# A column roll of an 8192 x 8192 matrix: which of the last rows are copied as half rows

## The chip, the cores and the metric

The kernel runs on one core of one Trainium2 chip. The metric is the device time of one execution in microseconds (us), taken as the median over several executions; lower is better. A profiled execution also leaves a page and a trace, from which the busy times, waits and DMA records here are read.

## The reference

The matrix is float32, 268 MB, and every row is rotated to the right by 100 columns:

```python
def setup_inputs():
    return {
        "x": np.random.randn(8192, 8192).astype(np.float32),
        "shift": 100,
    }

def reference(x: np.ndarray, shift: int) -> np.ndarray:
    return np.roll(x, shift, axis=1)
```

So `out[r, 100:] = x[r, :8092]` and `out[r, :100] = x[r, 8092:]`. Nothing is computed; the kernel only moves data, 268 MB read and 268 MB written.

## The kernel before

With a shift of 100 the kernel sets `a = 256` and `g = a - s = 156` (lines 20 to 23). Output columns from 256 on go one way, the first 256 columns another.

*The wide part (lines 34 to 43).* Columns 256 to 8191 of the output are copied straight from DRAM to DRAM. The rows are viewed as 128 blocks `c` of 64 rows; a block's rows are numbered by `e` (16) and `j` (4), and a DMA takes one `c` and one `j`: sixteen rows, four rows apart, each a contiguous run of 7936 floats (31,744 bytes, "a whole row" in this text). Such a DMA moves 496 KB. Even `j` are issued on SP's queue, odd `j` on ACT's (`engines[j % 2]`, lines 25 and 43), two DMAs per block on each.

In the last four blocks, 256 rows, line 40 cuts the columns at `mid = (256 + 8192) // 256 * 128 = 4224`, and each group of sixteen rows goes as two DMAs of 3968 columns (15,872 bytes per row, 248 KB per DMA: "half rows"), one after the other on the same queue:

```python
for c in range(blocks):
    parts = ((a, mid), (mid, n_cols)) if c >= blocks - 4 and a < mid else ((a, n_cols),)
    for j in range(4):
        for lo, hi in parts:
            engines[j % 2].dma_start(out=om[c, j, :, lo:hi], in_=xm[c, j, :, lo - s:hi - s])
```

Each queue issues 248 whole-row and 16 half-row DMAs. The framework gives each queue four semaphores, which it uses in turn, and lets a DMA wait until the one that used its semaphore before has landed: each queue has at most four DMAs in flight, and the one issued fifth waits for the first. A DMA of sixteen rows puts one row on each of the sixteen DMA engines; its semaphore is full when all sixteen have marked their row complete.

*The edge part (lines 60 to 80).* The first 256 output columns are gathered in SBUF: for 16 groups of 512 rows, GpSimd's queue loads the pieces from both ends of the rows (lines 72, 73, 76), the vector engine copies them into place (lines 74, 77), and GpSimd's queue stores them (line 80). Nothing links this part to the wide part but the DMA engines, which both use.

At the end SP waits for all outstanding DMAs, and the engines meet at closing barriers.

Of the kernel before, what the change touches and what calls it, by code (L numbers as in the profile page):

```python
# [1 line left out]

# [4 lines left out]


@with_exitstack
def kernel(  # L10
    ctx: ExitStack,
    tc: tile.TileContext,
    x: bass.AP,
    shift: int,
    out: bass.AP,
):
    nc = tc.nc
    n_rows, n_cols = x.shape
    s = shift % n_cols
    a = -(-s // 128) * 128  # L20
    if 0 < a <= 384 and a + 128 <= n_cols:
        a += 128
    g = a - s
    P = nc.NUM_PARTITIONS
    engines = [nc.sync, nc.scalar]
    n_chunks = 16
    rows = n_rows // n_chunks

    xm = x.rearrange("(c e j) w -> c j e w", e=16, j=4)
    om = out.rearrange("(c e j) w -> c j e w", e=16, j=4)
    if a < n_cols:
        blocks = n_rows // 64
        mid = (a + n_cols) // 256 * 128
        for c in range(blocks):
            parts = ((a, mid), (mid, n_cols)) if c >= blocks - 4 and a < mid else ((a, n_cols),)  # L40
            for j in range(4):
                for lo, hi in parts:
                    engines[j % 2].dma_start(out=om[c, j, :, lo:hi], in_=xm[c, j, :, lo - s:hi - s])
    if a == 0:
        return


    if a > 512:
        for i in range(n_chunks):
            r = slice(i * rows, (i + 1) * rows)  # L50
            nc.gpsimd.dma_start(out=out[r, :s], in_=x[r, n_cols - s:])
            if g > 0:
                nc.gpsimd.dma_start(out=out[r, s:a], in_=x[r, :g])
        return

    Q = 4  # L60
    n_st = n_rows // (P * Q)
    reads = ctx.enter_context(tc.tile_pool(name="reads", bufs=n_st))
    heads = ctx.enter_context(tc.tile_pool(name="heads", bufs=n_st))
    xt = x.rearrange("(k p q) c -> k p q c", q=Q, p=P)
    ot = out.rearrange("(k p q) c -> k p q c", q=Q, p=P)
    tiles = []
    for k in range(n_st):
        t = reads.tile([P, Q - 1, a], x.dtype)
        h = heads.tile([P, Q, a], x.dtype)
        lead = bass.AP(tensor=x.tensor, offset=(k * P * Q + 1) * n_cols - s,  # L70
                       ap=[[Q * n_cols, P], [n_cols, Q - 1], [1, a]])
        nc.gpsimd.dma_start(out=t[:], in_=lead)  # L72
        nc.gpsimd.dma_start(out=h[:, Q - 1, :s], in_=xt[k, :, Q - 1, n_cols - s:])  # L73
        nc.vector.tensor_copy(h[:, :Q - 1, :s], t[:, :, :s])  # L74
        if g > 0:
            nc.gpsimd.dma_start(out=h[:, 0, s:], in_=xt[k, :, 0, :g])  # L76
            nc.vector.tensor_copy(h[:, 1:, s:], t[:, :, s:])  # L77
        tiles.append(h)
    for k, h in enumerate(tiles):
        nc.gpsimd.dma_start(out=ot[k, :, :, :a], in_=h[:])  # L80


# [1 line left out]
_INS = ['x', 'shift']  # L84
_OUTS = [((8192, 8192), 'float32')]

_NUMBERS = {'shift': 100}


# [26 lines left out]
```

## Time and profile before

| what | value |
|---|---|
| median of 4 runs | 828.56 us (828.01, 828.45, 828.67, 831.01) |
| the profiled execution's own time | 828.13 us |
| its span, first to last instruction | 826.3 us |
| HBM read and written | 268.44 MB each |
| busy: GpSimd, vector engine | 41.1 us, 12.0 us |
| last issue of the edge part's stores | 401 us |
| issue of one DMA on SP's queue, on ACT's | 0.51 us, 0.52 us |
| first half-row DMA issued, last one | 793.3 us, 819.7 us |

The profiled execution is one run of the program, and its own time is 1.8 us above its span. The page shows the load of the DMA engines as tenths per fortieth of the span, and per stretch as a share: 1.00 means that all sixteen are moving data all the time. The GB/s beside it count each byte once, as read from its source. The trace holds a record of each packet that a DMA engine moved (here a packet is a row or a half row), with its start, duration, queue and size, and for each DMA sixteen completion marks, one from each DMA engine.

### The profile page before, as it was taken

To read this page: it belongs to the slowest core of one execution; us is meant where nothing else is said; L and a number is where in the kernel's file an instruction comes from. 1 tells how busy PE (TensorE), PEld (TensorE's weight loads), DVE (VectorE), ACT (ScalarE), POOL (GpSimd) and SP (SyncE) were. 2 spreads that over 40 slices of the span, in tenths; PEclk is the share of its full clock that TensorE was granted. 3 is DMA by queue.
4 is the path that set the end of the run, shared out by engine and by line. 5 is a ranking of instruction groups with operands and counts; after the bars stand their busy time and mean duration, and the time that the engine had idled before them with its cause. 6 is when DMAs were issued, how large, how long until landed. Compare 5 with 4: busy or idle time off the path is not lost. (4 is left out here: it accounts for less than half of the span.)

```text
span 826.3 us, 689 instructions
## 1 busy us (share of the span) xinstructions
DVE 12.0 (1%) x32; POOL 41.1 (5%) x68
## 2 busy tenths in 40 slices
DVE  0000000000000000000000000000000000000000
POOL 2001100010011000000000000000000000000000
DMA  9999999999999999999999999999999999999998
GB/s 305 349 328 354 346 343 335 345 336 343 343 342 351 354 350 351 349 346 350 345 353 339 325 328 332 329 327 335 323 335 318 331 322 337 326 321 333 327 310 288
DMA packets 22277, 276.90 MB, mean 335 GB/s; under 512 B 9472, under 2 KB 9728, under 8 KB 13824
## 3 DMA queue, kind: packets, MB, share of 16 engines
q1 hardware_dynamic: 8448, 130.04, 46.3%
q10 hardware_dynamic: 8448, 130.04, 44.5%
q0 software_dynamic: 5376, 16.78, 8.3%
q14 instruction: 5, 0.04, 0.0%
HBM read 268.44 MB, written 268.44 MB: 650 GB/s over the span
## 5 line engine op out<-in xcount | busy, mean ns | idle before, releaser
L80 POOL DMA_DIRECT2D out_dram<-h x16 | 11.4, 713 | 143.6 <-DMA out_dram<-h 84.5
L76 POOL DMA_DIRECT2D h<-in_x_dram x16 | 8.7, 541 | 148.1 <-DMA t<-in_x_dram 148.1
L72 POOL DMA_DIRECT2D t<-in_x_dram x16 | 12.2, 760 | 29.2 <-DMA h<-in_x_dram 28.3
L73 POOL DMA_DIRECT2D h<-in_x_dram x16 | 8.9, 558 | 40.3 <-DMA h<-in_x_dram 40.3
L74 DVE COPY h<-t 128x300 f32<-128x300 f32 x16 | 5.9, 367 | 277.0 <-DMA t<-in_x_dram 277.0
L77 DVE COPY h<-t 128x468 f32<-128x468 f32 x16 | 7.5, 468 | 0.0
L97 POOL MEMSET const-float32-0.0<- 128x1 f32 x1 | 0.1, 98 | 0.2 <-issue 0.2
L97 POOL MEMSET const-bfloat16-1.0<- 128x1 bf16 x1 | 0.1, 101 | 0.0
L97 POOL MEMSET const-uint8-127<- 128x1 uint8 x1 | 0.1, 99 | 0.0
L97 POOL MEMSET const-float32-1.0<- 128x1 f32 x1 | 0.1, 98 | 0.0
## 6 DMA issues: line engine op xcount, KB each, us to landing
out_dram<-in_x_dram ACTq DMA_DIRECT2D x248, 496.0 KB, 12.7
out_dram<-in_x_dram SPq DMA_DIRECT2D x248, 496.0 KB, 12.7
out_dram<-h POOLq DMA_DIRECT2D x16, 512.0 KB, 97.9
t<-in_x_dram POOLq DMA_DIRECT2D x16, 384.0 KB, 51.3
out_dram<-in_x_dram SPq DMA_DIRECT2D x16, 248.0 KB, 6.0
out_dram<-in_x_dram ACTq DMA_DIRECT2D x16, 248.0 KB, 6.0
h<-in_x_dram POOLq DMA_DIRECT2D x16, 78.0 KB, 43.2
h<-in_x_dram POOLq DMA_DIRECT2D x16, 50.0 KB, 50.0
```

Source lines behind the costliest of these rows:

```text
L72: nc.gpsimd.dma_start(out=t[:], in_=lead)
L73: nc.gpsimd.dma_start(out=h[:, Q - 1, :s], in_=xt[k, :, Q - 1, n_cols - s:])
L74: nc.vector.tensor_copy(h[:, :Q - 1, :s], t[:, :, :s])
L76: nc.gpsimd.dma_start(out=h[:, 0, s:], in_=xt[k, :, 0, :g])
L77: nc.vector.tensor_copy(h[:, 1:, s:], t[:, :, s:])
L80: nc.gpsimd.dma_start(out=ot[k, :, :, :a], in_=h[:])
L97: nc = _bacc.Bacc("TRN2", target_bir_lowering=False, num_devices=1)
```

## The change

Half rows are kept for the last two groups of sixteen rows alone: in the last block, for `j` of 2 (SP's queue) and 3 (ACT's queue). Blocks 124 to 126 and `j` of 0 and 1 in block 127 go as whole rows. Columns, rows per DMA, queues and the edge part are as before. Each queue now issues 255 whole-row and 2 half-row DMAs.

```diff
         for c in range(blocks):
-            parts = ((a, mid), (mid, n_cols)) if c >= blocks - 4 and a < mid else ((a, n_cols),)
             for j in range(4):
+                last = c == blocks - 1 and j >= 2 and a < mid
+                parts = ((a, mid), (mid, n_cols)) if last else ((a, n_cols),)
                 for lo, hi in parts:
                     engines[j % 2].dma_start(out=om[c, j, :, lo:hi], in_=xm[c, j, :, lo - s:hi - s])
```

## The prediction

> **What bounds the kernel now.** I read the busy shares and the forty slices first, then the queues and issues, then the waits of the SP queue, then a table of stretches over the end, and last the packet and completion records of the trace.
>
> ```profile
> span 826.3 us, 689 instructions
> DVE 12.0 (1%) x32; POOL 41.1 (5%) x68
> DMA  9999999999999999999999999999999999999998
> ...
> q1 hardware_dynamic: 8448, 130.04, 46.3%
> q10 hardware_dynamic: 8448, 130.04, 44.5%
> q0 software_dynamic: 5376, 16.78, 8.3%
> ```
>
> No compute engine is above 5%, and the sixteen DMA engines are busy in every slice: the kernel is a copy, bound by what these engines move. q1 and q10 are the hardware queues of SP and ACT and carry 130 MB each; q0, GpSimd's, has only the edge columns and lands its last store at 510.9 us, long before the rows that the change touches.
>
> ```profile
> out_dram<-in_x_dram ACTq DMA_DIRECT2D x248, 496.0 KB, 12.7
> out_dram<-in_x_dram SPq DMA_DIRECT2D x248, 496.0 KB, 12.7
> out_dram<-in_x_dram SPq DMA_DIRECT2D x16, 248.0 KB, 6.0
> out_dram<-in_x_dram ACTq DMA_DIRECT2D x16, 248.0 KB, 6.0
> ```
>
> A whole-row DMA lands 12.7 us after its issue, a half-row one after 6.0 us. Each has sixteen rows, one per DMA engine. Each queue keeps four in flight: an issue waits for the landing of the DMA four earlier on its queue. The SP issue at 793.33 us, for one, follows by 0.02 us the last of the sixteen completion marks of the DMA on whose semaphore it waits.
>
> ```profile
> engine line waited for: us in total, times, longest us
> SPq L43 <- DMA out_dram<-in_x_dram: 18.1, 14, 2.5
> SPq L111 <- DMA out_dram<-in_x_dram: 5.2, 4, 2.2
> ```
>
> These are the SP queue's waits from 795 to 827 us. A DMA counts as landed when the slowest engine has done its row, so that engine sets the pace of issue, and faster ones eat into what they still have queued.
>
> ```profile
> 700.00:780.00 80.00, 0.00 (x0) 0.00 (x0) 1.00 1.00 326
> 780.00:800.00 20.00, 0.00 (x0) 0.00 (x0) 1.00 1.00 327
> 800.00:805.00 5.00, 0.00 (x0) 0.00 (x0) 1.00 0.83 276
> 805.00:810.00 5.00, 0.00 (x0) 0.00 (x0) 1.00 0.94 330
> 810.00:815.00 5.00, 0.00 (x0) 0.00 (x0) 1.00 0.97 318
> 815.00:820.00 5.00, 0.00 (x0) 0.00 (x0) 1.00 0.96 333
> 820.00:823.00 3.00, 0.00 (x0) 0.00 (x0) 1.00 1.00 328
> 823.00:824.00 1.00, 0.00 (x0) 0.00 (x0) 1.00 0.58 222
> 824.00:825.00 1.00, 0.00 (x0) 0.00 (x0) 1.00 0.08 32
> ```
>
> The last two columns are DMA share and GB/s. Whole rows run at share 1.00 and 326 to 327 GB/s. Where half rows take over there is a dip (0.83, 276 GB/s), then a share of 0.94 to 0.97 at nearly the old rate, then a drain of about one microsecond.
>
> The sixteen completion marks of each DMA explain the dip. For the DMA that landed at 793.31 us, the marks stand before the last one by 7.2, 5.2, 4.9 ... 2.0, 1.7 and 0 us, 3.7 us on the mean. I call this the mean lag: how far the slowest engine is behind the average. From 500 to 795 us it lies between 3.5 and 5.6 us, mean 4.3. Under half rows it shrinks, since what a queue holds for an engine is halved and the fast engines run empty while the slowest catches up: 1.7 us on the mean after 800 us, 0.90 us for the last DMA, which lands at 825.38 us. The span ends 0.97 us later, after the closing barriers.
>
> **The change, part by part.** Blocks 124 to 126 and the first two row groups of block 127 become whole rows. That removes 28 half-row DMAs and adds 14 whole ones; 4 half ones stay, one pair at the end of each queue.
>
> *Issues.* Each queue issues 7 fewer DMAs of 0.51 us, 3.6 us in all. They lie beside the movement of bytes: SP alone waited 18.1 us for landings in that stretch. Worth 0 as long as landings set the pace; were that cover gone, the saving would be 3.6 us at the most, but the wait row excludes it.
>
> *Packets.* A whole row's packet took 1.546 us on the mean from 700 to 795 us (979 packets, shortest 1.173), a half row's 0.736 us (512 packets, shortest 0.589). Twice the half is 1.47 us, so a whole row is no cheaper per byte; it looks 0.07 us dearer. Fourteen rows per engine change: 14 x 0.074 = 1.0 us if that is a property of size, 0 if it comes from fewer engines being active at a time (shares of 0.94 to 0.97). The rates, 326 against 318 to 333, speak for the second; I take 0 and keep 1.0 for the range.
>
> *The dip goes.* From 800 to 823 us the rows above moved 5 x (276 + 330 + 318 + 333) + 3 x 328 = 7269 units where 327 throughout would give 7521; the 252 missing are 0.77 us. They are gained.
>
> *The lag stays to the end.* The work saved there must be paid in the drain: the slowest engine keeps its lag and ends alone. Its price I work out by two routes.
>
> First route, by the pace of the slowest engine. Until SP's issue at 802.15 us the two kernels are paced by the same whole-row landings. After that SP issues the two DMAs of block 126, the whole one of block 127 and its two halves: five steps. Ten steps took 793.31 - 762.74 = 30.57 us, so five take 15.3, and the last issue comes at 817.4. Then each queue holds two whole and two half rows for the slowest engine, six rows' worth in all: 6 x 1.546 = 9.3, landing at 826.7 if the engines crowd each other to the end. They don't: the others are 3.7 us, or 2.4 rows, ahead and finish first. Alone, the slowest engine did pairs of half rows in 1.18, 1.20 and 1.18 us (landings at 802.14, 803.32, 804.52 and 805.70), so 1.18 per row's worth. That takes off 2.4 x (1.546 - 1.18) = 0.9: 825.8, against 825.38 before. **+0.4 us.**
>
> Second route, by bytes. The average engine ended at 825.38 - 0.90 = 824.48. Without the dip it ends 0.77 earlier, 823.7. The slowest follows after its lag, worked off alone: 3.7 x 1.18 / 1.546 = 2.8. It lands at 826.5. **+1.1 us.**
>
> The lag could end smaller (1.7 us, as under half rows: -0.4 by the second route) or larger (5.6 us: 4.3 in the drain, +2.6). Five steps from 600 to 700 us took between 14.58 and 16.68, which by the first route gives -0.3 to +1.8. The routes use the same lag in opposite ways, so I take their middle, **+0.75 us**. The four halves left at the very end save nothing: the fast engines can run empty only once all has been issued.
>
> *The sum.* Profiled execution: 828.13 us, of which 826.3 is span; 0 + 0 + 0.75 makes 828.9. The median of the runs shown is 828.56, 0.43 above the profiled one, so the predicted time is **829.3 us**, +0.09%. A difference under 0.3% (2.5 us) is what a measurement of this kernel can hardly tell from none; its four runs went from 828.01 to 831.01.
>
> One rule speaks against this sum. The Trainium skill, page "DMA: Bandwidth & Descriptors", section "Anatomy of one DMA", fits, for DMAs that GpSimd issues, a fixed 2.0 us each plus the bytes over 436 GB/s, and its "Rules for kernel authors" ask for few, large DMAs. By it 14 fewer DMAs would save an estimated 28 us one after the other, or 3.5 us with eight in flight, and the kernel would take some 825 us. The rates of half and whole rows above show no such fixed part on this path: with eight DMAs in flight it is hidden, and the trace decides.
>
> **The rivals.**
>
> *Relief alone.* The dip was pure loss, and two half pairs are enough to close the lag. For it: the mean lag fell from 3.0 to 1.2 us between the landings at 803.33 and 806.34, within four steps. Against: that took eight half rows issued while the slowest was working off its backlog; here the last four are all in flight at once. It gives -0.77: 827.8.
>
> *Size.* Whole rows are really dearer by 0.07 us each. For it: 0.736 against 1.546. Against: the equal rates. It adds 1.0 to the middle: 830.3.
>
> *A long drain, on the slower side.* One mechanism: the slowest engine's lag at the last issue. Where whole rows stay, nothing pulls it back before the end. For it: the mean lag was 4.8 us from 650 to 700 us and up to 5.6 for single DMAs. Against: 3.4 to 4.2 us from 750 to 797 us. At a lag of 5.6 the second route gives +2.6: 831.2. It passes 0.3% from a lag of about 5.5 us on, or earlier where whole rows are dearer as well.
>
> *The change doesn't do what it says.* As built, each queue has 255 whole-row DMAs and 2 half-row ones where it had 248 and 16, in the order of the loop, and the same four semaphores in turn; no wait is new. I give this nothing.
>
> **How the numbers follow.** The middle (829.3): 0.50, own range 828.2 to 830.6, of which 0.48 is within 0.3% and 0.02 slower. Relief alone (827.8): 0.19, of which 0.02 is faster by over 0.3%. Size (830.3): 0.12, of which 0.03 slower. Long drain (831.2): 0.17, of which 0.14 slower. Left over, a different order of slow engines over the run: 0.02, half faster, half slower. Together: faster 0.03, within 0.77, slower 0.20. The range from 827.6 to 831.6 takes in the relief and most of the long drains.
>
> **What would show it.** Right: the dip at the turn to half rows is gone and share and rate stay at 1.00 and about 327 to some 820 us; 14 whole DMAs more, 28 half ones fewer; the drain with falling share is 2 to 4 us long instead of one; the last DMA's mean lag is 2 to 3.5 us; the last issue stands near 817 us. Wrong: a rate from 700 us on that differs by more than 1%, which no step here moves; a lag under 1.5 us at the end (relief); or a last landing after 828 us (long drain).

## The result, and the profile after

The changed kernel took 830.09 us (median of 48 runs, 827.13 to 833.87) against 828.93 us for the kernel before (69 runs): a ratio of 1.0013, with a 95% interval of 1.0006 to 1.0019. That is 1.1 us more (0.5 to 1.6); 0.75 us were predicted. The two medians are themselves 1.16 us apart. The profiled execution took 829.63 us with a span of 827.85 us; the profiled execution before had a span of 826.35 us.

The changed kernel's page, the issues of its wide part:

```profile
out_dram<-in_x_dram SPq DMA_DIRECT2D x255, 496.0 KB, 12.7
out_dram<-in_x_dram ACTq DMA_DIRECT2D x255, 496.0 KB, 12.7
...
out_dram<-in_x_dram SPq DMA_DIRECT2D x2, 248.0 KB, 8.9
out_dram<-in_x_dram ACTq DMA_DIRECT2D x2, 248.0 KB, 8.9
```

Whole rows land as before, 12.7 us after issue. The last two pairs of half rows take 8.9 us where half rows took 6.0: whole rows are still queued ahead of them.

Its table of stretches over the end (the last two columns are DMA share and GB/s):

```profile
800.00:805.00 5.00, 0.00 (x0) 0.00 (x0) 1.00 1.05 349
805.00:810.00 5.00, 0.00 (x0) 0.00 (x0) 1.00 1.00 305
810.00:815.00 5.00, 0.00 (x0) 0.00 (x0) 1.00 0.98 343
815.00:820.00 5.00, 0.00 (x0) 0.00 (x0) 1.00 1.02 308
820.00:823.00 3.00, 0.00 (x0) 0.00 (x0) 1.00 0.76 275
823.00:824.00 1.00, 0.00 (x0) 0.00 (x0) 1.00 0.69 270
824.00:825.00 1.00, 0.00 (x0) 0.00 (x0) 1.00 0.49 206
825.00:826.00 1.00, 0.00 (x0) 0.00 (x0) 1.00 0.12 48
826.00:827.90 1.90, 0.00 (x0) 0.00 (x0) 1.00 0.00 0
```

The dip of 0.83 at 800 to 805 us is gone: from 800 to 820 the share is 0.98 to 1.05, and the rate 326 GB/s on the mean. (A packet's time and bytes are counted where it starts, so short stretches swing and can pass 1.00.) In its place the share falls from 820 us on; the drain lasts some six microseconds. Before, the share was still 1.00 at 820 to 823 us, and the drain took one to two.

The last DMA's sixteen completion marks, worked out from the trace, show how unevenly the engines end. Each number is by how many us a mark stands before the last one:

```
before:  1.3 1.3 1.3 1.2 1.2 1.0 1.0 1.0 1.0 1.0 0.8 0.7 0.6 0.6 0.2 0.0   mean lag 0.90, landing 825.38
changed: 3.8 3.7 3.1 2.8 2.0 1.9 1.8 1.1 1.1 1.1 1.0 0.7 0.5 0.2 0.0 0.0   mean lag 1.56, landing 826.51
```

In the changed kernel some engines are done almost four microseconds before the last ones. The last ones are not one engine alone: two stand at 0.0 us and a third at 0.2. The landing is 1.13 us later, of the 1.5 us by which the spans differ. The rest comes after the landing: 826.346 - 825.385 = 0.96 us before, 827.851 - 826.510 = 1.34 us now. The SP queue's waits of the changed kernel, from 795 us on, show where:

```profile
engine line waited for: us in total, times, longest us
SPq L44 <- DMA out_dram<-in_x_dram: 20.0, 8, 3.3
SPq L112 <- DMA out_dram<-in_x_dram: 7.8, 1, 7.8
```

The closing wait (line 112, line 111 before) was four waits of 5.2 us in total; now it is a single one of 7.8 us. SP goes through the eight semaphores of the two queues in a fixed order. In the kernel before, the last DMAs use the last ones, so all but the last two waits are over when they land. With 257 DMAs per queue, one more than a multiple of four, the last DMA uses the first semaphore: SP stands at the first wait until 826.53 us and takes the other seven after it, the last at 826.97.

### The profile page after: what moved, and what is told of

Same layout as the page of the kernel before. It is cut to its first block, busy times and chain, and to the rows that moved or that the text cites. A ratio compares the mean times of both kernels' runs of the same rounds, so it can differ in the third digit from the quotient of the medians.

```text
span 827.9 us, 675 instructions
## 1 busy us (share of the span) xinstructions
DVE 12.0 (1%) x32; POOL 41.2 (5%) x68
## 5 line engine op out<-in xcount | busy, mean ns | idle before, releaser
L81 POOL DMA_DIRECT2D out_dram<-h x16 | 11.4, 720 | 121.6 <-DMA out_dram<-h 90.2
## 6 DMA issues: line engine op xcount, KB each, us to landing
out_dram<-in_x_dram SPq DMA_DIRECT2D x255, 496.0 KB, 12.7
out_dram<-in_x_dram ACTq DMA_DIRECT2D x255, 496.0 KB, 12.7
t<-in_x_dram POOLq DMA_DIRECT2D x16, 384.0 KB, 40.7
```

## The experiments

They ran on three chips, and in each set of runs the kernel before takes 817.4 to 817.8 us, against 828.93 us in the runs of the result. Ratios are to the kernel before in the same set of runs, with 95% intervals; 0.001 is 0.8 us. Each lag comes from the one profiled execution of its run. The diffs are against the changed kernel and show the lines that matter; `...` stands for lines left out.

**No half rows at all.**

```diff
-                last = c == blocks - 1 and j >= 2 and a < mid
-                parts = ((a, mid), (mid, n_cols)) if last else ((a, n_cols),)
+                parts = ((a, n_cols),)
```

> No half rows at all. Lag theory (half rows work only by halving what is queued, which pulls the slowest DMA engine back; the last two pairs come too late for that): like the changed kernel, 1.001 to 1.002 of before; the last DMA's mean lag 2 to 4 us, the drain with falling DMA share 3 to 6 us. Relief theory (the last pairs alone close the lag): clearly over the changed kernel, 1.003 or more. Size theory (a whole row is 0.07 us dearer than two halves): 1.001 to 1.002 too, so this run doesn't tell it from the lag theory.

Measured: 818.34 us, 1.0015 (1.0003 to 1.0027). The last DMA's mean lag was 2.25 us; its stretches at the end:

```profile
805.00:810.00 5.00, 0.00 (x0) 0.00 (x0) 1.00 0.99 337
810.00:812.00 2.00, 0.00 (x0) 0.00 (x0) 1.00 0.47 190
812.00:814.00 2.00, 0.00 (x0) 0.00 (x0) 1.00 0.52 222
```

The same as the changed kernel within the intervals, which are about a microsecond wide on either side. If the two pairs that the change keeps do anything, it is less than these runs resolve. The relief theory, by which these pairs close the lag and this run lands at 1.003 or more, falls.

**Half rows first instead of last.**

```diff
-                last = c == blocks - 1 and j >= 2 and a < mid
-                parts = ((a, mid), (mid, n_cols)) if last else ((a, n_cols),)
+                parts = ((a, mid), (mid, n_cols)) if c < 4 else ((a, n_cols),)
```

> The first 256 rows go as half rows, all others whole: the same DMAs as in the kernel before, the half ones at the other end of the run. Lag theory: the drain of whole rows, 1.001 to 1.002 of before, last DMA's mean lag 2 to 4 us. Size theory: 1.000, as the number of half rows is that of before.

Measured: 818.9 us, 1.0018 (1.0002 to 1.0034), last mean lag 3.34 us. The same DMAs as before, of the same lengths and in the same number, cost more with the half ones at the start: their place decides, not their number or size. (Half rows at the start also change how the edge part gets on, see the last section; the run before this one and the next have no half rows there and say the same.)

**The last 256 rows as half rows, 32 rows to a DMA.** Packets as before, bytes in flight as with whole rows.

```diff
+        xe = x.rearrange("(c e j) w -> c e j w", e=16, j=4)
+        oe = out.rearrange("(c e j) w -> c e j w", e=16, j=4)
         for c in range(blocks):
+            if c >= blocks - 4:
+                for h in range(2):
+                    for lo, hi in ((a, mid), (mid, n_cols)):
+                        engines[h].dma_start(out=oe[c, :, 2 * h:2 * h + 2, lo:hi], in_=xe[c, :, 2 * h:2 * h + 2, lo - s:hi - s])
+                continue
...
```

(`xe` and `oe` are the same rows in another order: a DMA takes, for each of the sixteen `e`, two neighbouring rows, and still leaves sixteen completion marks, so each engine has two rows of it. All other rows go whole. `xe` and `oe` are made in the same way in the other runs that use them.)

> The last 256 rows as half rows, but 32 rows to a DMA: the packets of the kernel before, the bytes in flight of whole rows. Lag theory: no dip at the turn, the lag stays, last DMA's mean lag 2 to 4 us, 1.001 to 1.002 of before like the changed kernel. If short packets are what helps at the end: 1.000.

Measured: 818.78 us, 1.0014 (1.0004 to 1.0024), last mean lag 2.89 us, no dip (shares of 0.98 to 1.01 from 790 to 810 us), as the lag theory had it. Short packets alone don't help at the end; what helped before was the smaller amount queued.

**Half rows everywhere, sixteen and 32 rows to a DMA.**

```diff
-                last = c == blocks - 1 and j >= 2 and a < mid
-                parts = ((a, mid), (mid, n_cols)) if last else ((a, n_cols),)
+                parts = ((a, mid), (mid, n_cols))
```

> Every group of sixteen rows goes as two half-row DMAs, four in flight per queue as before, so half the bytes in flight over the whole run. Lag theory: mean lag 1 to 2 us throughout, DMA share 0.94 to 0.97, rate within 2% of whole rows, 0.99 to 1.02 of before, no drain beyond 1.5 us. Size theory: 496 more rows per engine cheaper by 0.07 us each, 37 us off, 0.956 of before.

Measured: 820.6 us, 1.0041 (1.0023 to 1.0058). The lag behaves as expected: mean 1.02 us from 500 to 795 us, 0.38 us at the end. But there is no lasting loss of share (1.00 from 200 us on), which I had expected at 0.94 to 0.97, and the kernel is slower, not 4% faster.

```diff
         for c in range(blocks):
...
+            for h in range(2):
+                parts = ((a, mid), (mid, n_cols))
                 for lo, hi in parts:
...
+                    engines[h].dma_start(out=oe[c, :, 2 * h:2 * h + 2, lo:hi], in_=xe[c, :, 2 * h:2 * h + 2, lo - s:hi - s])
```

> Half rows everywhere, but 32 rows to a DMA (two half rows per engine), so packets are half as long and the bytes in flight are those of whole rows. Lag theory: mean lag 3 to 5 us as with whole rows, a long drain, 1.000 to 1.004 of before. Size theory: 0.956 of before.

Measured: 822.4 us, 1.0056 (1.0038 to 1.0075), mean lag 4.2 us, at the end 3.4. The size theory (0.956, or 782 us) falls in both runs by over 35 us. The lag follows the bytes in flight, not the packet's length. The median is worse than the 1.004 I allowed (the interval begins at 1.0038), so short packets seem to cost something.

**Half rows for the last 4096 rows, sixteen and 32 rows to a DMA.**

```diff
-                last = c == blocks - 1 and j >= 2 and a < mid
+                last = c >= blocks // 2 and a < mid
```

> Half rows for the last 4096 rows, all of them after the bulk of the edge part, so that this run is little touched by how the DMA engines share their time with GpSimd's queue. Lag theory: one dip at the turn, then a mean lag near 1 us at the rate of whole rows, 0.998 to 1.002 of before. Size theory: 240 more rows per engine at 0.07 us less each, 18 us off, 0.979.

Measured: 820.64 us, 1.0048 (1.0030 to 1.0066), outside what the lag theory gave, though the lag was short (1.1 us, at the end 0.59). The next run looks for what made it slow.

```diff
-            if c >= blocks - 4:
+            if c >= blocks // 2:
```

(This against the run with 32 half rows to a DMA in the last 256 rows.)

> The last 4096 rows as half rows, 32 rows to a DMA: short packets for half the run, with the bytes in flight of whole rows; the run with the same rows sixteen to a DMA took 1.0048. If short packets are dear in themselves: 1.004 to 1.006, and a rate from 540 to 790 us under that of whole rows by 0.5%. If the halved bytes in flight made that run slow: 1.001 to 1.002, with the drain of whole rows and their rate. Size theory of the prediction: 0.979.

Measured: 820.63 us, 1.0034 (1.0022 to 1.0047), last mean lag 3.22 us. It lies between the two expectations. From 540 to 790 us, with only the wide part running, the rates don't settle it: 333 GB/s for all whole rows and 331 for whole rows in the run with half ones first, against 330 and 331 in these two and 332 and 332 with half rows everywhere. In time, the four runs with many half rows are all slower, 1.0034 to 1.0056 against 1.0015 for none. Where the drain is as long as with whole rows, 32 half rows to a DMA everywhere against none, the difference is 0.0041 x 818 = 3.4 us (1.6 to 5.2 by the intervals) over 512 rows per engine, about 7 ns for each row cut.

The packet records settle the size theory. From 540 to 790 us, with all engines busy, a whole row's packet takes 1.502 to 1.520 us on the mean (the runs with no half rows, with the half rows first, with 32 half rows to a DMA at the end, and the repeat of the changed kernel); a half row's takes 0.753 to 0.759 (the four runs with many), so two halves take 1.505 to 1.518, the same. On an engine that works alone, a whole row takes 1.175 us (the last eight rows of the next run) and a half row 0.592 (the last ones in the repeat of the changed kernel), so two halves are dearer by 9 ns, not cheaper by 70. For the 14 rows per engine of the change that is 0.1 us, in the other direction than the size theory had it. It doesn't explain all of the 1.0048 for sixteen half rows to a DMA in the last 4096 rows, since 256 rows per engine at 9 ns are 2.3 us and the short drain should give back most of that. The rest stays open.

**Whole rows, 32 to a DMA**, to make the lag larger; and the same **with the last 256 rows as in the kernel before**.

```diff
         for c in range(blocks):
...
+            for h in range(2):
+                engines[h].dma_start(out=oe[c, :, 2 * h:2 * h + 2, a:], in_=xe[c, :, 2 * h:2 * h + 2, g:n_cols - s])
```

> Whole rows throughout, 32 rows to a DMA, so twice the bytes in flight and no half rows at the end. Lag theory: the slowest engine may fall further behind, mean lag 5 to 9 us, and all of it is paid in the drain: 1.003 to 1.008 of before. If the drain is not what sets the end: within 0.2% of the changed kernel's 1.0013.

```diff
         for c in range(blocks):
+            if c < blocks - 4:
+                for h in range(2):
+                    engines[h].dma_start(out=oe[c, :, 2 * h:2 * h + 2, a:], in_=xe[c, :, 2 * h:2 * h + 2, g:n_cols - s])
+                continue
             for j in range(4):
...
+                for lo, hi in ((a, mid), (mid, n_cols)):
                     engines[j % 2].dma_start(out=om[c, j, :, lo:hi], in_=xm[c, j, :, lo - s:hi - s])
```

> As the run with 32 whole rows to a DMA, but the last 256 rows as in the kernel before: sixteen half rows to a DMA. Lag theory: the lag is pulled in at the turn, with a deeper dip than before, last DMA's mean lag under 2 us, and at least 2 us faster than the run without the half rows at the end. If half rows at the end don't matter: the same as that run.

Measured: 830.62 us, 1.0154 (1.0136 to 1.0173) without, and 827.69 us, 1.0117 (1.0095 to 1.0139) with half rows at the end. The end of the first of the two by stretches:

```profile
810.00:815.00 5.00, 0.00 (x0) 0.00 (x0) 1.00 0.92 330
815.00:820.00 5.00, 0.00 (x0) 0.00 (x0) 1.00 0.15 64
820.00:825.00 5.00, 0.00 (x0) 0.00 (x0) 1.00 0.06 25
825.00:829.30 4.30, 0.00 (x0) 0.00 (x0) 1.00 0.03 15
```

For ten microseconds one engine of sixteen works alone, and 1/16 is 0.06. The slowest stood 14.1 us behind the mean from 500 to 795 us, where I had expected 5 to 9, and 11.4 us at the last DMA; there the second slowest was 10 us ahead of it. The 1.54% are 12.6 us, also more than expected, and most of it is lag. Against the run without half rows, the last DMA lands 12.9 us later; 9.2 us of that is the larger mean lag (11.4 against 2.2), and by 3.7 us the engines ended later on the mean, for which no run here shows the cause. The second of the two, the same columns:

```profile
780.00:790.00 10.00, 0.00 (x0) 0.00 (x0) 1.00 1.00 340
790.00:795.00 5.00, 0.00 (x0) 0.00 (x0) 1.00 0.74 254
795.00:800.00 5.00, 0.00 (x0) 0.00 (x0) 1.00 0.60 222
800.00:805.00 5.00, 0.00 (x0) 0.00 (x0) 1.00 0.50 165
805.00:810.00 5.00, 0.00 (x0) 0.00 (x0) 1.00 0.70 225
810.00:815.00 5.00, 0.00 (x0) 0.00 (x0) 1.00 0.96 362
```

The lag, 10.5 us on the mean from 500 to 795 us in this execution, is pulled in at the turn to half rows and is 0.48 us at the end. The dip costs 5 x (75 + 107 + 164 + 104) = 2250 units against the 329 GB/s that this kernel ran at from 700 to 780 us, 6.8 us; the 362 GB/s after it bring back half a microsecond. So half rows at the end do not avoid the lag; they pay at the turn, here at half to three quarters of the rate, what would otherwise be paid with one engine running. Here that is cheaper by 0.0037, 3.0 us (0.7 to 5.4 by the intervals).

**A gentler step down.** Blocks 116 to 123 alternate whole and half rows, 124 to 127 are half, the last two groups quarter rows.

```diff
+        w = (n_cols - a) // 4
         for c in range(blocks):
             for j in range(4):
...
+                n = 1
+                if c >= blocks - 4:
+                    n = 2
+                elif c >= blocks - 12 and j >= 2:
+                    n = 2
+                if c == blocks - 1 and j >= 2:
+                    n = 4
+                for k in range(n):
+                    lo, hi = a + k * 4 * w // n, a + (k + 1) * 4 * w // n
                     engines[j % 2].dma_start(out=om[c, j, :, lo:hi], in_=xm[c, j, :, lo - s:hi - s])
```

> Blocks 116 to 123 alternate whole and half rows, 124 to 127 are half rows as in the kernel before, and the last two groups of sixteen rows go as quarter rows. Lag theory: a gentler step down in the bytes in flight closes the lag while enough engines stay busy to hold the rate, so the dip is shallower than 276 GB/s over 5 us and the last DMA's mean lag is under 0.9 us: 0.9985 to 1.0000 of before. If the cost of closing the lag is the same however it is spread: 1.0000 to 1.0005.

Measured: 818.05 us, 1.0007 (0.9998 to 1.0015), last mean lag 0.41 us. The dip came at 745 to 750 us instead, no shallower, with 273 GB/s at a share of 0.78, and a small one (298 GB/s) at 770 to 775. The median lies above both expectations and the interval reaches over both, so the time doesn't tell them apart; the dip speaks against the first. The run shows no gain over the kernel before.

**The changed kernel again**, and then **with 260 DMAs per queue instead of 257**.

> The changed kernel once more, on a chip where others were measured. Lag theory: 1.0006 to 1.0019 of before as on record, last DMA's mean lag 1.5 to 3 us, drain of 3 us or more.

Measured: 819.46 us, 1.0018 (1.0009 to 1.0027), last mean lag 2.71 us, from the last landing to the end of the span 1.35 us: as on record, with a longer lag than in the first profile.

```diff
-                last = c == blocks - 1 and j >= 2 and a < mid
+                last = c in (100, 101, 102, blocks - 1) and j >= 2 and a < mid
```

> The changed kernel, with three more groups per queue as half rows near 650 us, so that each queue issues 260 DMAs, a multiple of its four semaphores, where the changed kernel has 257. If the closing waits, which go through the semaphores in a fixed order, cost more because the last DMA uses the first one: from the last landing to the end of the span 0.95 us as before, where the changed kernel had 1.34. The drain and the mean lag stay those of the changed kernel; against before 1.0003 to 1.0018, some 0.4 us under the changed kernel, which these runs can't resolve. If the closing has another cause: 1.3 us again.

Measured: 819.35 us, 1.0025 (1.0012 to 1.0038), last mean lag 2.74 us, from the last landing to the end 0.96 us. The SP queue's closing waits, first of the repeated changed kernel, then of this one:

```profile
SPq L112 <- DMA out_dram<-in_x_dram: 8.2, 1, 8.2
```

```profile
SPq L112 <- DMA out_dram<-in_x_dram: 6.9, 4, 2.5
```

One wait has become four again, and 0.39 us are gone after the landing. The trace shows this term; the medians, whose intervals are some 0.1 to 0.25% wide, can't, and here the median even lies above what I had expected (1.0018 at the most). The other runs agree, and so does one that was not made for it: from the last landing to the end it is 0.89 to 0.90 us where the DMA that lands last uses the eighth semaphore in the order of the waits, 0.95 to 0.96 us where it uses the seventh, 1.13 us where it uses the fourth (the gentler step down, 274 DMAs per queue), and 1.34 to 1.35 us where it uses the first (the changed kernel and its repeat). Each wait that SP still has to take costs about 0.06 us.

## Why the prediction was right

*The forecast.* +0.09% was forecast, +0.13% (0.06 to 0.19) measured, within the 0.3% that the likeliest case held.

*The dip goes: right; the 0.77 us gained: not seen in this profile.* The changed kernel runs at 326 GB/s from 800 to 820 us. But the average engine ended at 826.51 - 1.56 = 824.95 us, where the second route had 823.7 and the kernel before 824.48. A single execution can't tell a gain of this size: the four runs before the change already differ by 3 us.

*The lag is paid in the drain: right, and shown from both sides.* Half rows at the other end of the run, none at all, or with twice the rows per DMA all give 1.0014 to 1.0018. With the lag at 11 us the price is 12.6 us, most of it lag.

*The size of the lag: of the right order, and not steady.* The second route put the slowest engine 2.8 us behind the mean at the end. It was 1.56 us in the changed kernel's profile, under the 2 to 3.5 named as a sign of being right and just above the 1.5 that would have spoken for relief. The repeat had 2.71, the other whole-row endings 2.25 to 3.34, so the sign holds for the kernel, if not for its first profile. The drain was longer than the 2 to 4 us forecast, since several engines fell idle early.

*"[T]he slowest engine keeps its lag and ends alone": only in part.* Two engines ended together in the changed kernel's profile, and at 824 to 825 us half of them were still moving data (share 0.49). The pace of 1.18 us per row was read where the slowest engine was not alone either (share 0.83 from 800 to 805 us); it holds all the same, since a row on a lone engine took 1.175 us.

*The landing: right, with luck.* It came at 826.51 us, 826.5 by the second route. That sum met it by two misses that cancel: the average engine ended 1.2 us later than forecast, and the lag was 1.2 us smaller. By the first route the last SP issue was to come at 817.4 and the landing at 825.8; the issue came at 818.17, 0.8 us later, and the landing 0.7 us later.

*The four half rows at the end save nothing: not contradicted.* Without them the ratio is 1.0015; a saving under about a microsecond would not show.

*The closing: wrong.* "[T]he same four semaphores in turn; no wait is new. I give this nothing" overlooked where the turn ends. 257 is not a multiple of four; the closing waits start with the semaphore that fills last, and about 0.38 us are added after the landing. Of the 1.5 us between the two spans that is a quarter. That 0.75 + 0.38 = 1.13 comes out at the 1.1 us measured is worth little: the measured interval is 0.5 to 1.6.

*Packets at 0: right.* Whole rows seemed 0.07 us dearer than two halves by mean packet time, but the half rows' mean of 0.736 us came from a stretch in which fewer engines were active (shares of 0.83 to 0.97 from 800 to 820 us). With all engines busy two halves took 1.505 to 1.518 us and a whole row 1.502 to 1.520, and the difference is gone.

*Half rows at a share of 0.94 to 0.97: not lasting.* With half rows everywhere they move at a share of 1.00 from 200 us on. The lower share belongs to the turn: with half rows for the last 4096 it is 0.96 from 420 to 500 us, soon after the turn, and 0.99 to 1.00 after that. My expectation for that run copied it too far.

## What to carry to other kernels

A DMA that spreads over sixteen engines lands with the slowest, and in these runs the slowest fell behind by a good part of what was kept in flight. The lag was paid where the queues ran out: at the end, or where less is put in flight. Cutting the last transfers helped, by 0.14 to 0.18% here, when it halved what was in flight for the last 256 rows; one final pair per queue showed no gain, and part of what the cut pulls in is paid at the turn. Before calling a size dear by its mean packet time, compare stretches in which equally many engines are busy. Look also at which semaphore the last transfer uses and in what order the closing waits go through them.

## What the runs showed of the hardware

The lag grows faster than what is in flight. By the completion marks from 500 to 795 us:

```
rows in flight per engine   kernel                                          mean lag, us
 4 (8 half rows)            half rows everywhere, or in the last 4096       1.0, 1.1
 8                          before, changed, its repeat                     4.3, 4.2, 3.9
                            none half, half first, 32 half rows at the end  3.5, 4.5, 3.4
 8 (16 half rows)           32 to a DMA, everywhere, or in the last 4096    4.2, 4.2
16                          whole rows, 32 to a DMA, without, with half end 14.1, 10.5
```

With 16 rows in flight it is mostly one engine: the second slowest is 8.9 and 3.5 us ahead of the slowest, on the mean. With 8 whole rows the second slowest is only 0.3 to 2.0 us ahead, so it is not one engine alone. Whether it is always the same engines, and what makes them slow, these runs don't tell: the records don't name the engine.

An engine's pace depends on how many others are busy. A whole row took 1.175 us on an engine that worked alone (the last eight rows of the run with 32 whole rows to a DMA) and 1.50 to 1.55 us on the mean with all sixteen busy (the kernels that send whole rows, after 540 us).

What the two hardware queues keep queued also changed how the DMA engines share their time with GpSimd's. The median times to landing of the edge part's larger loads, of all whole rows and then of half rows everywhere:

```profile
t<-in_x_dram POOLq DMA_DIRECT2D x16, 384.0 KB, 53.2
```

```profile
t<-in_x_dram POOLq DMA_DIRECT2D x16, 384.0 KB, 18.1
```

The edge part lands its last store at 181.3 us instead of 530.4. Kernels that send whole rows, sixteen to a DMA, until 600 us vary here (40.7 to 54.3 us, and 469.5 to 530.4), but not by so much. It is not packet length alone: with the same half rows, 32 to a DMA, the loads take 35.7 us and the last store lands at 362.3; with whole rows, 32 to a DMA, it is 72.5 us and 737.5. Shorter packets and less in flight on the other queues both let GpSimd's work through. With half rows everywhere the first 180 us move 365 GB/s against 340, and yet the kernel gains nothing as a whole: the rest of the run is left with the wide part alone, at about 332 GB/s.
